# The gates' exponentials moved behind the last convolution activation, the parameter load put first, and two gate rows written in place by VectorE

## The chip, the cores and the metric

The kernel runs on one core of one Trainium2 chip. The metric is the device time of one execution in microseconds (us); lower is better. A core has five engines with queues of their own: TensorE (PE in the profile; its weight loads are PEld), VectorE (DVE), ScalarE (ACT), GpSimd (POOL) and SyncE (SP), which issues most of the transfers. Each engine works through its queue in order, and waits on semaphores for the others.

## The reference

One layer of a hybrid decoder for a prompt of 512 tokens and a sample group of 8 sequences of 8 tokens, which share the weights (576 tokens of width 1024 in all). The layer adds three blocks to x, each with RMS norms around it: a mixer with Mamba-2 heads and mLSTM heads behind one combined input projection, a cross attention to a memory, and a SwiGLU block. The part that matters here is the mixer's beginning:

```python
u = _rms(x) * g_pre_mix
proj = u @ w_in
z, xbc, dt_raw, q, k, v, ig, fg, og = jnp.split(proj, split_at, axis=-1)
xbc, conv_new = causal_conv(xbc, conv_buf, conv_w, conv_b)
xbc = jax.nn.silu(xbc)
dt = jax.nn.softplus(dt_raw.astype(jnp.float32) + dt_bias.astype(jnp.float32))
a = -jnp.exp(a_log.astype(jnp.float32))
y_ssd, h_new = ssd_scan(xs, dt, a, bm, cm, h_ssm)
...
logf = jax.nn.log_sigmoid((fg + b_fgate).astype(jnp.float32))
h_ml, c_new, n_new, m_new = mlstm_scan(q, k, v, i_pre, logf, mc, mn, mm)
```

Both scans go chunk by chunk. Inside them stand running sums of the gates' logarithms (cum, and the mLSTM's running maximum), and exponentials of differences of these sums: decays from a step to its chunk's end, and of a chunk as a whole.

## The kernel before

All of the work is in one function, `build`, over tiles of 128 partitions; features lie on the partitions and the 576 tokens along the free axis. A product of float32 matrices is made of three products of halves: each operand is split into a rounded part and its rest (`uh` and `ul` for the input, `whi` and `wlo` for the weights), and TensorE adds whi·uh, whi·ul and wlo·uh in PSUM (lines 208, 209 and 211 in the helper, 350 to 352 for the first two tiles). Weights come by transfer into `raw`, ScalarE casts them to `whi` (L186), and `wlo` is made by VectorE (L193) or by ScalarE and an accumulating transfer of GpSimd (L190, L191).

**The order.** Most of the program's order on each engine is chosen by the scheduler of the tile framework, which simulates a timeline (`TCOPT = dict(schedule_with_timeline_sim=True)`). Each engine then runs that fixed order. `tc.issue_after(x)` adds an edge that keeps the block's instructions on x's engine behind x in that order, and `tc.high_priority` raises a block's rank. Tiles come from pools with a fixed number of buffers; `MP` takes its PSUM banks from a pool of three, `GP` from another pool of three.

**The start.** VectorE clears `wz`, and TensorE runs `NWARM` = 17 products of 128x256 in bfloat16 on it, whose results nobody reads. Meanwhile SP issues the first transfers in this order: a piece of weights `raws[0]` (L318), the parameters `par` (L320: gains, biases, convolution weights), then the rows of x and further pieces of weights; the first row of x and the first piece of `raws[1]` go through ScalarE's queue. `uh` is x times a gain out of `par` (ScalarE, L333), `ul` the rest (VectorE, L334). The first two weight tiles are multiplied in step with the arrival of x, k by k; the third follows with its weights from L186 and L193.

**The convolution and the gates.** The projection's tiles come in the order: four convolution tiles, the gate tile, one q/k tile, eight more convolution tiles, seven more q/k tiles. `conv_tile` takes a tile out of PSUM (L469, L471), multiplies and adds the four taps (one ScalarE operation, L494, three of VectorE, L496) and ends with two Silu activations (L498, L500). The gate tile goes to `xg` (L448 to L452); from it a long row of VectorE operations makes softplus and the running sums: `pl`, `cum`, `mrw`, `mp`, `sx`, `gpr`. These are rows of 4 or 16 partitions and 576 columns. ScalarE copies them into one stack of rows, `r1`, which is cleared beforehand:

```python
    A.copy(r1[0:16, :], cum[0:16, :])
    A.copy(r1[32:48, :], pl[0:16, :])
    ...
    A.copy(r1[64:68, :], gpr[r4, :])
    A.copy(r1[96:100, :], sx[r4, :])
    A.copy(r2, mrw[r4, :])
```

TensorE transposes `r1` and `r2`, chunk by chunk, into the PSUM tiles `ps_ct` and `ps_ct2` (L589 to L594); copied out, they are `CT`, which has the gates by token. A product with a constant picks each chunk's last token (`ps_en`, L597; `ps_en2`, L604). Out of these come `wend`, `wendm`, `decp`, `scalem` and `expnm`, each by an exponential of ScalarE (L601 to L612). `decp` and `scalem` are read straight from `ps_en`. The whole of this stands under `tc.high_priority(offset=1000)`, so that in the schedule the exponentials stand among the Silus of the last convolution tiles.

**The state-space part.** `ssd_prompt` transposes B and x (`ps_bt`, `ps_xt`), multiplies B and C (`ps_cb`), and makes `xdt` (VectorE, L646), `xe` = `xdt` times `wend` (GpSimd, L650), the chunk states (`ps_h`, L652), the masks `lm` (L672 to L675) and the inner products (`ps_yi`, L682). The projection's q/k tiles, and after them the products of the value projection (`ps_v`, L854), fill TensorE's time between its steps. The list `steps_` ties these value products to steps of `ssd_prompt`: the first 33 stand behind the inner product of its third round.

Everything behind it (output projection, cross attention, SwiGLU) is touched by the change only through the time at which it starts.

Of the kernel before, what the change touches and what calls it, by code (L numbers as in the profile page):

```python
# [14 lines left out]
AF = mybir.ActivationFunctionType  # L15
ALU = mybir.AluOpType
# [4 lines left out]
T = 576  # L21
TP = 512
TS = 64
# [83 lines left out]

CUT = 512
CCUT = 128
NWARM = 17  # L110
NSS = 7
NWX = 3
TCOPT = dict(schedule_with_timeline_sim=True)
# [2 lines left out]
def build(nc, tc, ctx, I, O):  # L116
    V, A, G, S, TE = nc.vector, nc.scalar, nc.gpsimd, nc.sync, nc.tensor
# [35 lines left out]
    par = cp.tile([P, NPAR], F32, name="par")  # L153
# [139 lines left out]
    wendm = ml.tile([P, 5, 4], F32, name="wendm")  # L293
    scalem = ml.tile([P, 4, 4], F32, name="scalem")
# [12 lines left out]
    psw = MP("ps_warm")  # L307
    for _ in range(NWARM):
        mm(psw[:, 0:256], wz[:, 0:128], wz, start=True, stop=True, skip_group_check=True)

    wl = [wp.tile([P, 1024], F32R, name="wlo", tag="wlo", bufs=3) for _ in range(2)]
    RT = {k: wp.tile([P, 3], F32, name=k + "_r", tag=k + "_r") for k in ("px0", "p30", "px1", "p31")}
# [2 lines left out]
    for k in range(KT):  # L315
        if k % 2 == 0:
            c = slice(128 * k, 128 * k + 256)
            S.dma_start(raws[0][:, c], I["win"][1][:, c])  # L318
        if k == 0:
            S.dma_start(par, I["par"])  # L320
        xd = (S if k else A).dma_start(xraw[:, k, :], I["xT"][:, k, :])
        if k % 2 == 0:
            xd = (S if k else A).dma_start(raws[1][:, c], I["win"][2][:, c])
        if k == 0:
            with tc.issue_after(xd.ins), tc.high_priority(offset=300):

                A.activation(sp.tile([P, 1], F32, name="one"), wz[:, 0:1], AF.Exp)

        if k == 0:
            V.tensor_copy(wi[0][0][:, c], raws[0][:, c])  # L330
        for t0, n in ([(0, T)] if k else HALVES):
            ts_ = slice(t0, t0 + n)
            uhk = A.activation(uh[:, k, ts_], xraw[:, k, ts_], AF.Copy, scale=PAR("g_pre", k))  # L333
            ulk = V.scalar_tensor_tensor(ul[:, k, ts_], xraw[:, k, ts_], PAR("g_pre", k), uh[:, k, ts_].bitcast(F32),  # L334
                                         op0=ALU.mult, op1=ALU.subtract)
        if k % 2 == 0:
            for i in range(2):
                with tc.issue_after(uhk.ins), tc.issue_after(ulk.ins):
                    split(wi[i][0][:, c], wi[i][1][:, c], raws[i][:, c], cast=None if k or i else lambda *_: None)
# [81 lines left out]
    wend = bcp.tile([P, 5, 16], F32, name="wend")  # L421
    decp = bcp.tile([P, 4, 16], F32, name="decp")
# [35 lines left out]
    cst = cv.tile([P, 12, NB, 3], F32, name="cst")  # L458
    S.dma_start(cst, I["convst"])

    late_rows, last_in = [], [5]

    def conv_tile(j, dst):

        cb = cv.tile([P, 604], F32, name="cb", tag="cb", bufs=2)
        sm = cb[:, CS:CB].rearrange("p (b t) -> p b t", t=11)

        def ev(t0, n, ps):
            V.tensor_tensor(cb[:, 3 + t0:259 + t0], ps[:, 0:256], rxb[:, t0:t0 + 256], op=ALU.mult)  # L469
            if t0:  # L470
                V.tensor_tensor(sm[:, :, 3:11], ps[:, 256:320].rearrange("p (b t) -> p b t", t=8),  # L471
                                rxb[:, TP:T].rearrange("p (b t) -> p b t", t=8), op=ALU.mult)

        in_tile(1 + j, ev, CUT if j == 4 else 0)
        with ExitStack() as after:
            if 4 <= j < 10:
                for i in range(2 + j, 4 + j):
                    if i > last_in[0]:
                        fetch(i, 0)
                        last_in[0] = i  # L480
                after.enter_context(tc.issue_after(accs[-1].ins))
            if late_rows:
                late_rows.pop()()
            G.memset(cb[:, 0:3], 0.0)
            G.tensor_copy(sm[:, :, 0:3], cst[:, j, :, :])

        def rows_out():
            G.tensor_copy(convo[:, j, 0:3], cb[:, CS - 3:CS])
            G.tensor_copy(convo[:, j, 3:27].rearrange("p (b t) -> p b t", t=3), sm[:, :, 8:11])

        late_rows.append(rows_out)
        e = V
        ac = cv.tile([P, 604], F32, name="ac", tag="ac", bufs=2)
        A.activation(ac[:, 0:600], cb[:, 0:600], AF.Identity, scale=PAR("convw", 4 * j), bias=PAR("convb", j))  # L494
        for k in range(1, 4):
            e.scalar_tensor_tensor(ac[:, 0:600], cb[:, k:600 + k], PAR("convw", 4 * j + k), ac[:, 0:600],  # L496
                                   op0=ALU.mult, op1=ALU.add)
        A.activation(dst[:, 0:TP], ac[:, 0:TP], AF.Silu)  # L498
        sa = ac[:, CS:CB].rearrange("p (b t) -> p b t", t=11)
        A.activation(dst[:, TP:T].rearrange("p (b t) -> p b t", t=8), sa[:, :, 0:8], AF.Silu)  # L500


    qk = SL(1, "qk")
# [37 lines left out]
    r4 = slice(32, 36)  # L541
    r1 = row("r1", 100)
# [4 lines left out]
    i2, mrw, mp = row("i2"), row("mrw", tag="xg"), row("mp", tag="pl")  # L547
    l2, gpr = row("l2", tag="e1"), row("gpr", tag="rmask")
# [10 lines left out]
    V.tensor_copy(mp[r4, 512:576].rearrange("p (c t) -> p c t", t=8), m0.unsqueeze(2).to_broadcast([4, 8, 8]))  # L559
    sx = row("sx", tag="la")  # L560
    V.tensor_tensor(sx[r4, :], cum[r4, :], mrw[r4, :], op=ALU.subtract)
    sx_done = V.tensor_tensor(sx[r4, :], sx[r4, :], mp[r4, :], op=ALU.add)
    V.tensor_tensor(gpr[r4, :], ig[r4, :], cum[r4, :], op=ALU.subtract)
    V.tensor_tensor(gpr[r4, :], gpr[r4, :], mp[r4, :], op=ALU.subtract)
    r2 = row("r2", 4, tag="i2")
    A.copy(r1[64:68, :], gpr[r4, :])
    A.copy(r1[96:100, :], sx[r4, :])
    A.copy(r2, mrw[r4, :])
    V.tensor_copy(cdup, cum[0:16, TP:T].unsqueeze(1).to_broadcast([16, 2, TS]))
    A.copy(mrow, r2[:, TP:T])  # L570
# [2 lines left out]
    for st_, src, n in ((cumst, cum[0:16, :], 16), (sxst, sx[r4, :], 4)):  # L573
        b0 = 32 if n == 4 else 0
        bt, d1 = btt[b0:b0 + n, :], d1t[b0:b0 + n, :]
        G.memset(st_, 0.0)
        V.tensor_copy(bt, src)
        A.copy(st_[0:n, :], bt)
        with tc.issue_after(sx_done.ins):
            V.tensor_tensor(d1, src, bt, op=ALU.subtract)  # L580
        V.tensor_copy(bt, d1)
        A.copy(st_[32:32 + n, :], bt)
        V.tensor_tensor(d1, d1, bt, op=ALU.subtract)
        A.copy(st_[64:64 + n, :], d1)

    with tc.high_priority(offset=1000):
# [11 lines left out]
        en = pse[:, 0:416].rearrange("p (c k) -> p c k", c=4)  # L598
        V.tensor_tensor(wend[:, 0:4, :], en[:, :, 0:16], CT[:, 0:4, 0:16], op=ALU.subtract)
        V.tensor_tensor(wendm[:, 0:4, :], en[:, :, 96:100], CT[:, 0:4, 64:68], op=ALU.add)  # L600
        A.activation(decp, en[:, :, 0:16], AF.Exp)  # L601
        A.activation(scalem, en[:, :, 96:100], AF.Exp)
        pse = MP("ps_en2")
        mm(pse[:TS, 0:104], C32("esamp")[:TS, :], CT[:TS, 4, :], start=True, stop=True)  # L604
        V.tensor_tensor(wend[:TS, 4, :], pse[:TS, 0:16], CT[:TS, 4, 0:16], op=ALU.subtract)
        V.tensor_tensor(wendm[:TS, 4, :], pse[:TS, 96:100], CT[:TS, 4, 64:68], op=ALU.add)
        A.activation(wend[:, 0:4, :], wend[:, 0:4, :], AF.Exp)
        A.activation(wendm[:, 0:4, :], wendm[:, 0:4, :], AF.Exp)
        A.activation(wend[:TS, 4, :], wend[:TS, 4, :], AF.Exp)
        wd = A.activation(wendm[:TS, 4, :], wendm[:TS, 4, :], AF.Exp)  # L610
        with tc.issue_after(wd.ins):
            A.activation(expnm, CT[:, 0:4, 100:104], AF.Exp, scale=-1.0)  # L612
        V.tensor_scalar(ncum, CT[:, 0:4, 0:16], -1.0, None, op0=ALU.mult)
# [1804 lines left out]
```

## Time and profile before

| what | us |
|---|---|
| median of 3 executions | 1080.8 |
| lowest and highest | 1078.0, 1081.1 |
| profiled execution: its own time | 1079.13 |
| profiled execution: span, first to last instruction | 1077.4 |
| busy: TensorE | 1067.5 |
| busy: VectorE | 752.0 |
| busy: ScalarE | 607.8 |
| busy: GpSimd | 231.5 |

A row of the timeline has the start in us from the span's beginning, the time it took, the engine, the line, the operation, out<-in with shapes, and in brackets how long the engine had been idle and what ended that. A row of stretches has for each engine its busy time and, in brackets, the number of instructions, then TensorE's granted clock, the busy share of the transfer engines, and GB/s. A row of the chain has start, time, engine, tile, line and count. A row of the waits has who waited for whom, the sum in us, the times and the longest. Ends of products are modelled, so that products overlap in the records; their starts are what tells the rate.

### The profile page before, as it was taken

Reading aid. Unit: us, or ns where it says so; the run is one execution under the profiler, and the core shown is the slowest. Engines: PE = TensorE matmul, PEld = TensorE weight load, DVE = VectorE, ACT = ScalarE, POOL = GpSimd, SP = SyncE. Lnnn points to the kernel's source line nnn. Section 1 sums busy time; section 2 is a strip of 40 time slices with the busy share of each in tenths; the row PEclk is TensorE's granted clock in tenths of the full one; section 3 lists DMA queues with packets and bytes.
Section 4 is the critical chain, followed back from the end, with each engine's and each line's share of the span. In section 5 each row is a group of like instructions: output and inputs, shape, how many; then the busy total and the mean of one; then the engine's idle time right before and its main releaser. Section 6 shows DMA issues by size and latency. Waiting matters only on the chain.

```text
span 1077.4 us, 20699 instructions
## 1 busy us (share of the span) xinstructions
PE 1067.5 (99%) x8120; PEld 1015.1 (94%) x8120; DVE 752.0 (70%) x1509; ACT 607.8 (56%) x1094; POOL 231.5 (21%) x305
## 2 busy tenths in 40 slices
PE   9999999999999999999999999999999999999997
PEld 8999887778999999999999889999999999999997
DVE  6798775658877775559755555766467887787556
ACT  7778532345654555656555445645566566656653
POOL 0453643313213111000154301100011111111000
PEclk9999999999999999999999999999999999999998
DMA  6787544426655449743468775644476697588532
GB/s 208 164 171 133 159 127 177 147 73 183 191 153 145 111 120 329 254 169 109 147 206 286 268 257 176 241 131 93 136 181 140 155 201 167 116 190 184 130 132 89
DMA packets 58822, 181.76 MB, mean 169 GB/s; under 512 B 6588, under 2 KB 11836, under 8 KB 58212
## 3 DMA queue, kind: packets, MB, share of 16 engines
q1 hardware_dynamic: 42740, 138.06, 39.1%
q0 software_dynamic: 15408, 41.43, 20.0%
q8 instruction: 64, 1.05, 0.4%
q10 hardware_dynamic: 576, 0.95, 0.3%
q14 instruction: 34, 0.28, 0.1%
HBM read 159.75 MB, written 20.65 MB: 167 GB/s over the span
## 4 chain that ended last, share of the span: by engine, by line
PE 93%; DVE 3%; ACT 1%; DMA 1%; issue 1%; POOL 0%; DVEq 0%; SPq 0%; ACTq 0%
PE ps_in L208 6%; PE ps_in L211 6%; PE ps_in L209 6%; PE ps_v L854 5%; PE ps_o L211 3%; PE ps_g L1910 3%; PE ps_g L1909 3%; PE ps_o L209 3%; PE ps_g L1911 3%; PE ps_o L208 3%; PE ps_u L1910 3%; PE ps_u L1911 3%; PE ps_u L1909 3%; PE ps_dn L1909 2%; PE ps_dn L1910 2%; PE ps_dn L1911 2%
## 5 line engine op out<-in xcount | busy, mean ns | idle before, releaser
L211 PE MATMUL ps_in<-uh,wlo 128*128 128x320 f32 (+1 forms) x544 | 161.6, 298 | 0.0
L208 PE MATMUL ps_in<-uh,whi 128*128 128x320 f32 (+1 forms) x544 | 161.6, 297 | 0.0
L209 PE MATMUL ps_in<-ul,whi 128*128 128x320 f32 (+1 forms) x544 | 160.9, 296 | 0.0
L186 ACT CAST whi<-raw 128x1024 fp32r<-128x1024 f32 (+1 forms) x104 | 105.4, 1014 | 96.3 <-PE ps_in L209 30.2
L193 DVE TENSOR_TENSOR wlo<-raw,whi 128x1024 fp32r<-128x1024 f32 (+2 forms) x97 | 94.8, 979 | 61.8 <-ACT whi L186 57.3
L211 PEld LDWEIGHTS ps_in<-uh,wlo 128*128 128x128 f32 x544 | 102.2, 188 | 2.0 <-issue 1.3
L208 PEld LDWEIGHTS ps_in<-uh,whi 128*128 128x128 f32 x544 | 102.3, 188 | 1.5 <-issue 0.8
L209 PEld LDWEIGHTS ps_in<-ul,whi 128*128 128x128 f32 x544 | 102.3, 188 | 0.4
L191 POOL DMA_DIRECT2D wlo<-win x31 | 27.2, 876 | 76.0 <-ACT wlo L190 64.7
L1909 PE MATMUL ps_g<-b,whi 128*128 128x288 f32 x144 | 42.4, 295 | 0.0
L1910 PE MATMUL ps_g<-b,whi 128*128 128x288 f32 x144 | 42.4, 295 | 0.0
L1910 PE MATMUL ps_u<-b,whi 128*128 128x288 f32 x144 | 42.2, 294 | 0.0
L1909 PE MATMUL ps_u<-b,whi 128*128 128x288 f32 x144 | 42.2, 294 | 0.0
L1882 ACT CAST whi<-rawx 128x1024 fp32r<-128x1024 f32 (+1 forms) x26 | 25.7, 987 | 27.7 <-PE ps_dn L1910 13.7
L198 DVE TENSOR_TENSOR wlo<-sw,whi 128x1024 fp32r<-128x1024 f32 (+1 forms) x26 | 29.6, 1140 | 15.5 <-ACT whi L197 15.4
L208 PE MATMUL ps_xo<-qh,whi 128*128 128x288 f32 x128 | 38.4, 302 | 0.1
L211 PE MATMUL ps_o<-mixm_h,wlo 128*128 128x256 f32 (+1 forms) x128 | 37.7, 295 | 0.0
L209 PE MATMUL ps_xo<-ql,whi 128*128 128x288 f32 x128 | 37.7, 296 | 0.0
L209 PE MATMUL ps_o<-mixm_l,whi 128*128 128x256 f32 (+1 forms) x128 | 37.5, 293 | 0.0
L211 PE MATMUL ps_xq<-u2h,wlo 128*128 128x320 f32 (+1 forms) x128 | 37.5, 294 | 0.0
L209 PE MATMUL ps_xq<-u2l,whi 128*128 128x320 f32 (+1 forms) x128 | 37.4, 294 | 0.0
L211 PE MATMUL ps_o<-mixs_h,wlo 128*128 128x320 f32 (+1 forms) x128 | 37.4, 292 | 0.0
(770 smaller groups left out, 3848.6 us busy)
## 6 DMA issues: line engine op xcount, KB each, us to landing
raw<-win SPq DMA_DIRECT2D x35, 512.0 KB, 4.1
raw<-wout SPq DMA_DIRECT2D x17, 512.0 KB, 4.0
raw<-wxq SPq DMA_DIRECT2D x13, 512.0 KB, 4.0
raw<-wgate SPq DMA_DIRECT2D x13, 512.0 KB, 3.6
raw<-wup SPq DMA_DIRECT2D x13, 512.0 KB, 5.0
wlo<-win POOLq DMA_DIRECT2D x24, 256.0 KB, 5.1
kva<-vc SPq DMA_DIRECT2D x11, 512.0 KB, 6.5
raw<-wv SPq DMA_DIRECT2D x10, 512.0 KB, 4.1
```

The costliest lines, as they stand in the source:

```text
L186: casts.append(A.copy(hi[:, :n], raw[:, :n]))
L191: accs.append(G.dma_start(lo[:, a:b], src[:, a:b], accum_op=ALU.add))
L193: e.tensor_tensor(lo[:, a:b], raw[:, a:b], hi[:, a:b].bitcast(F32), op=ALU.subtract)
L198: (eng or V).tensor_tensor(lo, src, hi.bitcast(F32), op=ALU.subtract)
L208: mm(ps, wh, ah, start=i == 0, stop=False)
L209: mm(ps, wh, al, start=False, stop=False)
L211: m = mm(ps, tiles[order[c]][1], xh(order[c], t0, n), start=False, stop=c == len(tiles) - 1)
L854: mm(ps, a, b, skip_group_check=True, **kw)
L1882: A.copy(s.h3[:, s.all], s.r2[:, s.all])
L1909: mm(ps, wh, b[0][k], start=start and k == 0, stop=False, skip_group_check=True)
L1910: mm(ps, wh, b[1][k], start=False, stop=False, skip_group_check=True)
L1911: m = mm(ps, wl, b[0][k], start=False, stop=k == nk - 1, skip_group_check=True)
```

## The change

It has three parts. The transfer of `par` is issued on SP ahead of the first piece of weights instead of behind it, and there are 21 warm-up products instead of 17. The last step of `sx` and `gpr` is written by VectorE straight into `r1`, without ScalarE's two copies; `sx` itself, which a later stack of bfloat16 rows needs, is finished after that by one more VectorE operation, and the edge that held the bfloat16 stacks behind `sx` holds them behind the rows now. And the exponentials are put behind the last Silu in ScalarE's order: `decp` behind the last Silu, the others behind `decp`.

```diff
-NWARM = 17
+NWARM = 21
...
     for _ in range(NWARM):
         mm(psw[:, 0:256], wz[:, 0:128], wz, start=True, stop=True, skip_group_check=True)
+    S.dma_start(par, I["par"])
...
         if k % 2 == 0:
             c = slice(128 * k, 128 * k + 256)
             S.dma_start(raws[0][:, c], I["win"][1][:, c])
-        if k == 0:
-            S.dma_start(par, I["par"])
         xd = (S if k else A).dma_start(xraw[:, k, :], I["xT"][:, k, :])
...
-    late_rows, last_in = [], [5]
+    late_rows, last_in, silus = [], [5], []
...
         A.activation(dst[:, 0:TP], ac[:, 0:TP], AF.Silu)
         sa = ac[:, CS:CB].rearrange("p (b t) -> p b t", t=11)
-        A.activation(dst[:, TP:T].rearrange("p (b t) -> p b t", t=8), sa[:, :, 0:8], AF.Silu)
+        silus.append(A.activation(dst[:, TP:T].rearrange("p (b t) -> p b t", t=8), sa[:, :, 0:8], AF.Silu))
...
     V.tensor_tensor(sx[r4, :], cum[r4, :], mrw[r4, :], op=ALU.subtract)
-    sx_done = V.tensor_tensor(sx[r4, :], sx[r4, :], mp[r4, :], op=ALU.add)
+    V.tensor_tensor(r1[96:100, :], sx[r4, :], mp[r4, :], op=ALU.add)
     V.tensor_tensor(gpr[r4, :], ig[r4, :], cum[r4, :], op=ALU.subtract)
-    V.tensor_tensor(gpr[r4, :], gpr[r4, :], mp[r4, :], op=ALU.subtract)
+    r1_done = V.tensor_tensor(r1[64:68, :], gpr[r4, :], mp[r4, :], op=ALU.subtract)
+    with tc.issue_after(r1_done.ins):
+        V.tensor_tensor(sx[r4, :], sx[r4, :], mp[r4, :], op=ALU.add)
     r2 = row("r2", 4, tag="i2")
-    A.copy(r1[64:68, :], gpr[r4, :])
-    A.copy(r1[96:100, :], sx[r4, :])
     A.copy(r2, mrw[r4, :])
...
-        with tc.issue_after(sx_done.ins):
+        with tc.issue_after(r1_done.ins):
             V.tensor_tensor(d1, src, bt, op=ALU.subtract)
...
-        A.activation(decp, en[:, :, 0:16], AF.Exp)
-        A.activation(scalem, en[:, :, 96:100], AF.Exp)
+        with tc.issue_after(silus[-1].ins):
+            dx = A.activation(decp, en[:, :, 0:16], AF.Exp)
+        with tc.issue_after(dx.ins):
+            A.activation(scalem, en[:, :, 96:100], AF.Exp)
...
-        A.activation(wend[:, 0:4, :], wend[:, 0:4, :], AF.Exp)
-        A.activation(wendm[:, 0:4, :], wendm[:, 0:4, :], AF.Exp)
-        A.activation(wend[:TS, 4, :], wend[:TS, 4, :], AF.Exp)
-        wd = A.activation(wendm[:TS, 4, :], wendm[:TS, 4, :], AF.Exp)
+        with tc.issue_after(dx.ins):
+            A.activation(wend[:, 0:4, :], wend[:, 0:4, :], AF.Exp)
+            A.activation(wendm[:, 0:4, :], wendm[:, 0:4, :], AF.Exp)
+            A.activation(wend[:TS, 4, :], wend[:TS, 4, :], AF.Exp)
+            wd = A.activation(wendm[:TS, 4, :], wendm[:TS, 4, :], AF.Exp)
```

## The prediction

> **What bounds the kernel now.** I read the share of each engine first, then the waits of TensorE, then the same engine in stretches.
>
> ```profile
> PE 1067.5 (99%) x8120; PEld 1015.1 (94%) x8120; DVE 752.0 (70%) x1509; ACT 607.8 (56%) x1094; POOL 231.5 (21%) x305
> ```
> ```profile
> PE ps_warm L309 <- DVE wz L306: 1.1, 1, 1.1
> PE ps_in L350 <- ACT uh L333: 1.0, 1, 1.0
> PE ps_ct L589 <- ACT r L567: 0.3, 1, 0.3
> ```
> ```profile
> 0.00:10.00 10.00, 7.90 (x33) 6.32 (x34) 4.74 (x13) 5.52 (x11) 0.98 (x9) 1.00 0.83 257
> 10.00:20.00 10.00, 10.00 (x77) 10.00 (x77) 7.65 (x13) 7.69 (x13) 0.76 (x2) 1.00 0.89 300
> ...
> 1060.00:1077.40 17.40, 10.34 (x91) 10.05 (x89) 9.74 (x21) 5.51 (x12) 0.00 (x0) 0.84 0.33 118
> ```
> TensorE is busy for all but 9.9 of 1077.4 us. Of these, 7.1 lie in the last 17.4 us, which the change leaves alone; 2.1 lie ahead of the first real product and 0.3 at the gates' transposes ps_ct. Those last two places are the ones the change touches. No other engine's time counts unless TensorE waits for it. The second column of the stretches shows something else: 33 products in the first 10 us against 77 in the next, although TensorE is called busy in both. The reason is in the timeline of the start:
>
> ```profile
> 0.74 0.39 SPq L318 DMA_DIRECT2D raw<-win  x1
> ...
> 1.06 3.81 PE L309 MATMUL ps_warm<-wz 128*128 128x256 bf16 x17 [1.06 <-DVE wz L306]
> ...
> 4.50 0.29 DVE L330 CAST whi<-raw 128x256 fp32r<-128x256 f32 x1 [3.50 <-DMA raw<-win]
> ...
> 5.35 0.96 ACT L333 ACTIVATE uh<-xraw,par 128x256 fp32r<-128x256 f32 x2 [2.19 <-DMA par<-par]
> ...
> 5.91 1.09 PE L350 MATMUL ps_in<-uh,whi 128*128 128x256 f32 x2 [1.04 <-ACT uh L333]
> ...
> 7.01 0.41 PE L350 MATMUL ps_in<-uh,whi 128*128 128x256 f32 x1
> ...
> 7.23 0.41 PE L351 MATMUL ps_in<-ul,whi 128*128 128x256 f32 x1
> ...
> 13.38 0.28 PE L351 MATMUL ps_in<-ul,whi 128*128 128x256 f32 x1
> ...
> 13.49 0.28 PE L352 MATMUL ps_in<-uh,wlo 128*128 128x256 f32 x1
> ```
> The same 256 columns start 0.22 us apart at 7.0 (7.01, 7.23) and 0.11 us apart at 13.4 (13.38, 13.49): TensorE starts at half rate. The 17 warm-up products, 3.81/17 = 0.224 us each, were half rate throughout. Then it idled 1.04 us for the parameters, and it was still at half rate at 7.2.
>
> The Trainium skill, "TensorE: Matmul & The Clock Gate", Part 1, says that the clock goes to full rate only after a whole free-running window of about 3.4 us in which TensorE is busy. The trace agrees in that 3.81 us of work followed by a hole of 1.04 us was not enough; by the rule, unbroken work from 1.06 would reach full rate between 1.06 + 3.4 = 4.5 and 1.06 + 6.8 = 7.9, an estimate, and the gain would be the one worked out below, because its ceiling comes from elsewhere.
>
> **Edit 1: parameters first, 21 warm-up products.** The load of the parameters moves from second to first place on SP's queue, ahead of a weight load; the transfers behind keep their places.
>
> ```profile
> 1.19 4.07 DMA par<-par
> ```
> The parameters landed at 1.19 + 4.07 = 5.26, and ScalarE's first uh started at 5.35. Issued one place earlier, 0.45 us (1.19 less 0.74), I expect them at 4.8; if the input row, whose landing has no row, is later, the gain goes to 0. The weight load then lands 0.45 later, at 4.95 instead of 4.50, and its cast of 0.29 ends at 5.24, when uh is nearly ready too. Four more warm-up products cost 4 × 0.224 = 0.90 us and end at 1.06 + 21 × 0.224 = 5.76, against data for the first real product at about 5.45. They cost up to 0.3 us of waiting, but TensorE still starts 0.15 earlier than 5.91, and the hole of 1.04 is gone.
>
> What that brings: 33 − 17 = 16 real products took 5.91 to 10.0, 4.09 us; at the next stretch's 10/77 = 0.130 us they are 2.08 us. So full rate from the start is worth 2.0 us, and nothing if TensorE still speeds up as late as now. What is late next caps it:
>
> ```profile
> 17.33 1.23 DVE L193 TENSOR_TENSOR wlo<-raw,whi 128x1024 fp32r<-128x1024 f32 x1 [1.24 <-ACT whi L186]
> ```
> ```profile
> 20.61 0.31 PE L352 MATMUL ps_in<-uh,wlo 128*128 128x320 f32 x1
> ```
> The next unit's low weights are ready at 18.56, and TensorE comes for them at 20.61 + 0.15: they allow 2.2 at most, since they hang on a transfer and on ScalarE (the wait in their row), which do not move. I take 2.0, between 0 and 2.2.
>
> **Edit 2: two rows written by VectorE.** It removes two ScalarE copies and adds one VectorE operation (sx is still finished for its bfloat16 stack, but after the rows).
>
> ```profile
> 76.70 0.77 DVE L561 TENSOR_TENSOR sx<-cum,mrw 4x576 f32<-4x576 f32 x1
> ...
> 77.96 0.75 DVE L564 TENSOR_TENSOR gpr<-gpr,mp 4x576 f32<-4x576 f32 x1
> 78.74 0.84 DVE L496 SCALAR_TENSOR_TENSOR ac<-cb,par,ac 128x600 f32<-128x600 f32 x1
> ```
> ```profile
> 78.74 0.67 ACT L566 COPY r<-gpr 4x576 f32<-4x576 f32 x1 [1.18 <-DVE gpr L564]
> 79.44 1.05 ACT L186 CAST whi<-raw 128x1024 fp32r<-128x1024 f32 x1
> 80.52 0.67 ACT L567 COPY r<-sx 4x576 f32<-4x576 f32 x1
> ```
> ```profile
> 80.69 0.31 PE L208 MATMUL ps_in<-uh,whi 128*128 128x320 f32 x1
> 81.33 0.28 PE L589 MATMUL ps_ct<-c,r 100*128 100x100 f32 x1 [0.34 <-ACT r L567]
> ```
> Now the rows are whole at 80.52 + 0.67 = 81.19, and the transpose starts at 81.33, 0.64 after the product ahead of it, where 0.13 is usual (10/77, above): 0.5 us are lost. After the change VectorE needs two operations of 0.75 behind sx's end at 77.47: whole at 79.0, or at 80.3 with the convolution work that stands between them now (the 0.49 up to 77.96, and the 0.84 at 78.74). That is 0.9 to 2.2 earlier, so the 0.5 goes. But TensorE comes 2.0 earlier: if VectorE's chain started no sooner, it would wait 80.3 − 78.85 = 1.5 here. The chain's start, though, hung on TensorE:
>
> ```profile
> 39.55 0.43 ACT L448 COPY xg<-ps_in 40x320 f32<-40x320 f32 x1 [0.43 <-PE ps_in L445]
> ```
> so it moves most of the way with it. I take 0.4 of the 0.5; the bounds are +0.5 and −1.0. The added 0.75 on VectorE falls behind the rows; queued behind it are the convolution's multiply-adds (the 0.84 row is one), which nothing on TensorE waited for before; the same 0.75 is the most it can cost.
>
> **Edit 3: exponentials behind the last Silu.** The seven exponentials stand between two table loads, ahead of the last Silus:
>
> ```profile
> 91.45 1.28 ACT L607 ACT_TABLE_LOAD   x1
> ...
> 93.39 0.20 ACT L612 ACTIVATE expnm<-CT 128x16 f32<-128x16 f32 x1
> 93.59 1.28 ACT L498 ACT_TABLE_LOAD   x1
> ...
> 105.99 0.24 ACT L500 ACTIVATE xs<-ac 128x64 f32<-128x64 f32 x1
> ```
> ```profile
> 106.44 1.04 POOL L650 TENSOR_TENSOR xe<-xdt,wend 128x512 f32<-128x512 f32 x1 [0.71 <-DVE xdt L646]
> ```
> Two loads go, 2.56 us of ScalarE; the third, for the next exponential, only moves forward. TensorE does not wait for ScalarE here, so this is worth nothing by itself.
>
> The Trainium skill, "ScalarE: Activation LUTs", What ACT_TABLE_LOAD costs, gives about 2.66 us for each switch, with a drain; by it 5.3 us of ScalarE would go. The rows show 1.28 and the next exponential right behind, so the rows decide, and the sum is the same by both.
>
> The price is that wend, decp and scalem come after 106.23 + 1.28 + 0.3 to 0.9 = 107.8 to 108.4 instead of 93. The first reader is xe on GpSimd at 106.44, delayed 1.4 to 2.0. Behind the exponentials on ScalarE stand the copies of ps_bt and ps_cb and a cast of weights, up to 1.28 + 0.9 = 2.2 later; the first of them is the other operand of xe's product:
>
> ```profile
> 109.25 1.02 PE L652 MATMUL ps_h<-xe,btok 128*128 128x512 f32 x2
> ```
> xe ended at 107.48, 1.77 before this: the slack covers nearly all. Behind it the state-space chain feeds the value products, which are ordered behind its third inner product:
>
> ```profile
> 161.44 1.29 DVE L675 TENSOR_TENSOR lm<-lm,cbs 128x512 f32<-128x512 f32 x2
> ```
> ```profile
> 162.84 1.03 PE ps_yi L682 x16
> ...
> 164.91 2.09 PE ps_v L854 x9
> ```
> There the slack is 162.84 − 162.73 = 0.1, and the projection products that fill the gaps have just run out. Whatever the chain loses against TensorE beyond its slack becomes idle time: 0 to 2.0. I take 0.8, since the first link is covered and the last is not.
>
> **Sum**, against the profiled execution (1079.1 us, 1.7 more than its span): 2.0 + 0.4 − 0.8 = 1.6 off, 1077.5. The four executions known (1080.8, 1081.1, 1078.0, 1079.1) average 0.6 above that one, so I add 0.6: **1078.1**.
>
> **Rivals.** *All is kept (1076.0).* The chain moves with TensorE and the schedule fills around it: 2.0 + 0.5 off 1079.1 is 1076.6, and if speeding up late, by a varying amount, is also what makes the middle run 1.7 slower, up to 1.7 more comes off the runs: 1075 to 1076.6. For it: TensorE has no other wait. Against: the 0.1 at the third inner product. *TensorE does not speed up earlier, or VectorE's chain swallows it (1079.5).* Then the edits do not do what they say: 0 to 0.5 off the average, 1079.7. *Slower (1085): the bank of ps_en.* ps_en lies in one of three PSUM banks taken in turn (ps_ct, ps_ct2, ps_en, ps_en2, ps_bt, ps_cb), so ps_cb needs its bank, now held until decp and scalem are read.
>
> ```profile
> 99.43 1.06 PE L635 MATMUL ps_cb<-bc 128*128 128x128 f32 x8
> ```
> If the scheduler leaves ps_cb near 99.4, TensorE stands there until about 107.9, 8.5 us, and 2.4 off against 8.5 on gives 1085. It decides once ps_cb stands over 5.6 us ahead of the last exponential in true time (2.4 + 3.2). For it: TensorE is in order and everything queues behind ps_cb. Against: the order is made by a timeline simulation that knows the dependence, and its products came 1.8 us after their data at ps_h, so it is not optimistic here.
>
> **How the numbers follow.** A measurement of this kernel tells about 0.3%, 3.2 us, from no change: faster is below 1077.6, slower above 1084.0. The forecast has 0.45: a third of it falls below 1077.6 (0.15), the rest within. All kept 0.25, all of it faster. No earlier full rate 0.10, within. Slower 0.20, nearly all above 1084. Faster 0.40, same 0.40, slower 0.20. The range, 1074.5 to 1083.5, takes in the first three and leaves out most of the last.
>
> **What would show it.** Right: 21 warm-up products end where the first L350 starts, no wait on uh; products 0.11 us apart before 8 us; the first unit with L193's weights starts near 18.7; ps_ct released by VectorE with no wait; one table load between the Silus and the first exponential. Wrong: half rate still at 10 us; a new wait of ps_cb or ps_h on ScalarE, or idle TensorE ahead of the first ps_v.

## The result, and the profile after

The change made the kernel slower: 1086.65 us median of 6 runs (1084.88 to 1088.24) against 1079.27 for the kernel before (1077.57 to 1081.1), a ratio of 1.0068 with a 95% interval of 1.0054 to 1.0083. The forecast was 1078.1, its range ended at 1083.5. The profiled execution of after took 1087.2 us, its span 1085.4. One execution of one kernel further down, the repaired edit 2 without the exponentials, took 6024 us and is left out of the range given for it, though not out of its median.

TensorE is still busy for 99% of the span. Its waits, from the waits of after:

```profile
PE ps_hu L798 <- DVE h L799: 1.7, 1, 1.7
PE ps_hu L798 <- ACT bm L793: 1.4, 1, 1.4
PE ps_warm L309 <- DVE wz L306: 1.1, 1, 1.1
PE ps_os L1446 <- ACT kva L1471: 0.6, 1, 0.6
PE ps_in L208 <- ACT la L448: 0.6, 1, 0.6
PE ps_ct L588 <- DVE r L561: 0.6, 1, 0.6
PE ps_yi L684 <- DVE lm L677: 0.4, 1, 0.4
```

The wait for `uh` is gone. In its place stand five new ones, none of them in work that was edited, and the one at ps_ct has grown from 0.3 to 0.6. The start does what it was meant to do (timeline and stretches of after):

```profile
1.06 4.08 PE L309 MATMUL ps_warm<-wz 128*128 128x256 bf16 x21 [1.06 <-DVE wz L306]
4.10 0.96 ACT L332 ACTIVATE uh<-xraw,par 128x256 fp32r<-128x256 f32 x2
5.13 0.51 PE L349 MATMUL ps_in<-uh,whi 128*128 128x256 f32 x2
...
16.62 1.23 DVE L193 TENSOR_TENSOR wlo<-raw,whi 128x1024 fp32r<-128x1024 f32 x1 [1.56 <-ACT whi L186]
```
```profile
0.00:10.00 10.00, 8.94 (x57) 7.62 (x58) 5.35 (x13) 6.09 (x12) 0.98 (x9) 1.00 0.84 277
```

Real products begin at 5.13 instead of 5.91, and 57 products instead of 33 fall into the first 10 us (21 and 17 of them warm-up products). At the gates' transposes TensorE is 1.85 us ahead of before (79.48 against 81.33). The loss is made later. These are a stretch of before, and then two of after, around the first value products; the second column has TensorE's busy time and count, the first figure behind the last bracket its granted clock:

```profile
160.00:170.00 10.00, 10.00 (x67) 8.08 (x65) 7.32 (x16) 4.53 (x7) 1.03 (x1) 1.00 0.67 257
```
```profile
160.00:170.00 10.00, 7.82 (x45) 6.38 (x45) 8.44 (x19) 3.20 (x5) 1.01 (x1) 0.74 0.64 189
170.00:180.00 10.00, 10.00 (x46) 6.79 (x44) 5.61 (x14) 2.82 (x4) 1.20 (x2) 0.92 0.38 141
```

In after TensorE stands still for 2.2 us of the first stretch, and the clock falls in both. The timeline of TensorE shows it product by product, first the first value product of before, then after:

```profile
164.66 0.48 PE L854 MATMUL ps_v<-whi,uh 128*128 128x512 f32 x1
```
```profile
162.48 0.31 PE L211 MATMUL ps_in<-uh,wlo 128*128 128x320 f32 x1
164.53 0.56 PE L798 MATMUL ps_hu<-stb,bm 96*128 96x512 f32 x1 [1.74 <-DVE h L799]
165.53 1.98 PE L684 MATMUL ps_yi<-lm,xdt 128*64 128x128 f32 x16 [0.44 <-DVE lm L677]
...
169.06 0.77 PE L856 MATMUL ps_v<-whi,uh 128*128 128x512 f32 x1
169.63 0.63 PE L856 MATMUL ps_v<-whi,ul 128*128 128x512 f32 x1
170.05 0.63 PE L856 MATMUL ps_v<-wlo,uh 128*128 128x512 f32 x1
...
171.94 0.39 PE L856 MATMUL ps_v<-whi,ul 128*128 128x512 f32 x1
172.17 0.39 PE L856 MATMUL ps_v<-wlo,uh 128*128 128x512 f32 x1
```

The last projection product starts at 162.48. The next one, 2.05 us later, waited until VectorE had added an earlier product out of its PSUM bank to a state (its pool has two banks, and ps_hs holds one); the inner product behind it waited for a mask. The first value product comes at 169.06, where before, whose real products start 0.8 us later, had it at 164.66. And at 169.6 products of 512 columns start 0.42 us apart, at 172 0.23: after the idle time TensorE ran at half rate, from 164.82 to 171.64 by the record of the granted clock, 6.83 us in which half, 3.4 us, is lost.

A sum over the starts of all products between 20 and 1060 us (counting how much later each starts than the columns of the one ahead need at full rate, 512 columns in 0.23 us, where that is over 0.3 us) gives 8.1 us in after and 0.5 in before. So 7.6 us more idle and 3.4 lost at half rate, less 2.7 gained at the start (at ps_ss, 23.83 against 26.54, the best lead), make 8.3, where the spans differ by 8.0.

### The profile page after: what moved, and what is told of

The parts are those of the page before. It is cut to its first block, busy times and chain, and to the rows that moved or that the text cites. A ratio compares the mean times of both kernels' runs of the same rounds, so it can differ in the third digit from the quotient of the medians.

```text
span 1085.4 us, 20697 instructions
## 1 busy us (share of the span) xinstructions
PE 1071.6 (99%) x8124; PEld 1016.6 (94%) x8124; DVE 752.5 (69%) x1510; ACT 603.6 (56%) x1090; POOL 233.9 (22%) x305
## 4 chain that ended last, share of the span: by engine, by line
PE 83%; DMA 6%; DVE 5%; ACT 3%; issue 2%; POOL 0%; SPq 0%; DVEq 0%; ACTq 0%; POOLq 0%
PE ps_in L208 5%; PE ps_in L209 5%; PE ps_in L211 5%; PE ps_v L856 4%; PE ps_g L1912 3%; PE ps_u L1912 3%; PE ps_g L1911 3%; PE ps_u L1913 3%; PE ps_g L1913 3%; PE ps_u L1911 3%; PE ps_dn L1911 2%; PE ps_dn L1912 2%; PE ps_dn L208 2%; PE ps_dn L1913 2%; PE ps_dn L211 2%
## 5 line engine op out<-in xcount | busy, mean ns | idle before, releaser
L193 DVE TENSOR_TENSOR wlo<-raw,whi 128x1024 fp32r<-128x1024 f32 (+2 forms) x97 | 96.7, 999 | 62.7 <-ACT whi L186 61.6
L208 PE MATMUL ps_o<-mixm_h,whi 128*128 128x256 f32 (+1 forms) x128 | 37.4, 292 | 0.1
```

Of the source, the lines that this page charges most:

```text
L193: e.tensor_tensor(lo[:, a:b], raw[:, a:b], hi[:, a:b].bitcast(F32), op=ALU.subtract)
L208: mm(ps, wh, ah, start=i == 0, stop=False)
```

## The experiments

Each kernel was timed in five rounds beside the kernel before, whose medians in the three groups of runs were 1079.66, 1079.62 and 1079.64. After was timed in a group of its own, with 1079.27 for the kernel before, so a gain against after is some 0.4 us more than the two medians say. Ratios go by all runs and not by the medians alone.

**The three parts one by one.** Each diff of the change was applied alone, and the first two together.

> The kernel before with the first part alone: parameters first, 21 warm-up products. Theory A (the state-space chain sets the pace where the filling products run out): the start gives the 2.7 us that the changed kernel had gained at ps_ss, but the chain starts with the last Silu and does not move by as much, so part of it comes back as idle time ahead of the first ps_v: 1076.5 to 1079, and a wait of under 1.5 us there. Theory B (any change of the order shuffles the schedule and puts waits at places of no relation): anywhere from 1076 to 1084, with the waits elsewhere.

> The kernel before with the second part alone: two rows of r1 written by VectorE. Theory A: the wait of 0.5 us at ps_ct goes and nothing else changes, 1078.5 to 1079.5. Theory B: waits at new places, up to 4 us slower.

> The kernel before with the third part alone: the exponentials behind the last Silu. Theory A: the bank of ps_en is held some 13 us longer, ps_xt and with it the chain of states come later while TensorE runs ahead with projection products; these run out ahead of the third inner product, TensorE idles 1 to 3 us there and drops to half rate for up to 6.8 us: 1081.5 to 1085.5. Theory B: no idle time at that place, and the slower time of the change needs all three parts together.

> The changed kernel without its third part: first and second part together. Theory A: the start's gain and the rows' gain, less what the chain gives back: 1076 to 1078.5, no drop of the rate between 100 and 300 us. Theory B: as slow as the change, 1084 or more, if the first two parts alone shuffle the schedule so that the filling products run out.

| kernel | median us (range) | ratio to before, interval |
|---|---|---|
| edit 1, start | 1077.24 (1076.55 to 1079.56) | 0.9984, 0.9975 to 0.9993 |
| edit 2, rows | 1086.11 (1084.62 to 1087.42) | 1.0064, 1.0051 to 1.0077 |
| edit 3, exponentials | 1087.0 (1086.09 to 1088.46) | 1.0071, 1.0058 to 1.0085 |
| edits 1 and 2 | 1082.15 (1081.22 to 1084.48) | 1.0028, 1.0017 to 1.004 |

The start alone is a gain, the other two lose each by itself, and the losses do not add up. Edit 1 came out as both its theories allowed, edits 1 and 2 between their two. Edit 2 lost more than either of its theories had. Edit 3 showed what its theory A named, TensorE idle ahead of the third inner product (1.75 us up to 165.18, 0.50 up to 166.19) and half rate from 166.17 on, and took 1.5 us more than that theory's range.

Edit 1 leaves the order of all engines as it was behind the first few instructions, and its waits of TensorE are these, all of them:

```profile
PE ps_warm L309 <- DVE wz L306: 1.1, 1, 1.1
PE ps_in L208 <- ACT la L448: 0.3, 1, 0.3
PE ps_ct L588 <- ACT r L566: 0.2, 1, 0.2
```

Behind the start there is half a microsecond in which TensorE waits for anything. Whatever edits 2 and 3 do on VectorE and ScalarE, they had no more than that to gain. Both change the order that the scheduler chooses from the gates on: in the traces 138 of TensorE's 8120 products stand at another place with edit 2, 403 with edit 3. The new orders have waits. Edit 2 alone waits 0.8 us at ps_hu (to 177.90) and 1.2 at ps_yi (to 179.64), and has two windows of 3.41 us at half rate, from 84.26 and from 179.83. In edits 1 and 2, whose profile is 4.7 us longer than that of edit 1, the same two waits make 2.0 of it, a window of half rate at 82 us 1.7, and ps_ct 0.4.

Edit 2 alone, and edits 1 and 2, also have a change on ScalarE that nobody had asked for: the scheduler put a Silu between the exponentials, so that four table loads (1.28 us each) stand there instead of two. In edits 1 and 2 the last Silu starts at 107.99, with edit 1 alone at 104.38. What this adds to the lateness of the state-space part was not measured by itself.

**Is any new order a loss?** A copy that has no purpose was added to the kernel before:

```diff
+    A.copy(r1[96:100, :], sx[r4, :])
```

> The kernel before, with ScalarE's copy of the row sx into r1 done twice (0.67 us more on ScalarE, at the gates' transposes); nothing of the change is in it. The scheduler's order on TensorE differs from before in 27 places. Theory A (the loss needs the change's own work: late exponentials or rows): as before, 1079.7 within 1, apart from up to 0.7 at ps_ct; no waits of TensorE over 1 us between 160 and 215 us. Theory B (any disturbance of the scheduler's order loses, because the order before happens to have no waits): 1082 to 1087, with waits of ps_yi, ps_hu or ps_os that before does not have, and perhaps a window of half rate behind them.

1080.65 us (1079.27 to 1082.46), ratio 1.0011, 1.0002 to 1.002. In the traces the order on TensorE differs from that of before by more than with edit 2 (216 products, at 41 places; the expectation counted 27), and yet there is no wait of TensorE between 160 and 215 us. So not every new order loses. The kernel is a useful control for the next theory too, as the timeline of its VectorE and GpSimd shows:

```profile
145.25 4.63 DVE L676 TENSOR_TENSOR lm<-lm,cbs 128x512 f32<-128x512 f32 x2
```
```profile
145.04 9.51 POOL L794 TENSOR_TENSOR h<-h,vt 128x1024 f32<-128x1024 f32 x4 [2.59 <-PE ps_hs L786]
```

Two mask products take 4.63 us here, against 1.29 for two at 161.44 in before. They lie beside GpSimd's state products. TensorE had other work there and nothing waited.

**VectorE beside GpSimd.** In edits 1 and 2 together the fourth round's masks meet them, and there TensorE waits. In the experiment GpSimd's state products of the third round are held behind the masks; the order on the other engines stays the same but for single rows.

```diff
-                    G.tensor_copy(sd.tile([P, 1], F32, name="lm0"), lm[:, 0:1])
+                    held.append(G.tensor_copy(sd.tile([P, 1], F32, name="lm0"), lm[:, 0:1]))
...
-            with tc.issue_after(mults[7].ins) if b == 2 else ExitStack():
+            with tc.issue_after(held[0].ins) if b == 2 else ExitStack():
```

> Edits 1 and 2 without the exponentials, and GpSimd's two state products of the third round held behind the fourth round's mask, so that they no longer run beside VectorE's two mask products (2.23 and 1.82 us there, 0.68 each in before, where nothing ran beside them). The order of every other engine is that of edits 1 and 2. Theory C (two engines' contention makes the wait): the mask products take 0.7 each, the 1.7 us wait of ps_yi at 176 goes, the window of half rate at 82 stays, 1079 to 1080.8 beside 1082.2. Without contention: the mask products keep 1.8 to 2.2 and the time stays at 1082 to 1083, or is later still if the state is needed sooner than it comes now.

Edits 1 and 2 (timeline of VectorE, of GpSimd, of TensorE):

```profile
173.34 2.23 DVE L674 TENSOR_TENSOR lm<-lm,cbs 128x512 f32<-128x512 f32 x1
175.49 0.68 DVE L796 TENSOR_TENSOR h<-h,ps_hu 128x512 f32<-128x512 f32 x1
176.09 1.82 DVE L674 TENSOR_TENSOR lm<-lm,cbs 128x512 f32<-128x512 f32 x1
```
```profile
173.08 4.28 POOL L792 TENSOR_TENSOR h<-h,vt 128x1024 f32<-128x1024 f32 x2 [5.21 <-PE ps_hs L784]
```
```profile
177.96 1.09 PE L681 MATMUL ps_yi<-lm,xdt 128*64 128x128 f32 x16 [1.24 <-DVE lm L674]
```

With the state products held:

```profile
173.37 0.68 DVE L674 TENSOR_TENSOR lm<-lm,cbs 128x512 f32<-128x512 f32 x1
...
174.74 0.69 DVE L674 TENSOR_TENSOR lm<-lm,cbs 128x512 f32<-128x512 f32 x1
```
```profile
175.67 3.83 POOL L792 TENSOR_TENSOR h<-h,vt 128x1024 f32<-128x1024 f32 x2
```
```profile
175.64 1.09 PE L681 MATMUL ps_yi<-lm,xdt 128*64 128x128 f32 x16
```

The masks take 0.68 and 0.69 instead of 2.23 and 1.82, and the inner product starts at 175.64 instead of 177.96, without a wait. The median falls from 1082.15 to 1080.33 (1079.03 to 1081.91), as expected. Not all of that need be the masks'. The first profile has a window of half rate at 82 us, long before the edit can act; the second has none, came 1.5 us sooner to ps_xt, and then stood 1.1 us at ps_h. Executions with the same mean granted clock, 0.996, took 1081.61 to 1083.98 (four, edits 1 and 2) and 1080.33 and 1081.91 (two, held): on average 1.35 us less, about the 1.24 us that the inner product no longer waits. With so few executions this is a rough figure.

The rows show what the slowing depends on. The sum of the state at 175.49, in the middle of GpSimd's time, takes 0.68 as ever: one of its operands is in PSUM. The masks take both from SBUF. The Trainium skill, "SBUF — State Buffer", Who interferes with whom, says that a VectorE instruction with two SBUF inputs gets its second input through a read interface that it shares with GpSimd, and that the shared pair of ports is an exclusive lock. The trace agrees: the first of the two state products ran from 173.08 for its usual 1.94, to 175.02, and the mask of 173.34 ended at 175.57, 0.55 behind it; the second took 2.38, to 177.36, and the mask of 176.09 ended at 177.91, again 0.55 behind.

**The same in after.** There it is the weight casts of the value projection that meet GpSimd. This experiment leaves out fifteen of sixteen heads of the state products of the first two rounds:

```diff
-                G.tensor_tensor(hn, hn, decs[:, :, bb:bb + 1].to_broadcast([P, 16, 64]), op=ALU.mult)
+                nh = 1 if b < 2 else 16
+                G.tensor_tensor(hn[:, 0:nh, :], hn[:, 0:nh, :], decs[:, 0:nh, bb:bb + 1].to_broadcast([P, nh, 64]), op=ALU.mult)
```

> After, with GpSimd's four products of the sampled states of the first two rounds (128x1024 each, 9.4 us in all beside VectorE's two weight casts at 154.6) cut to one of their sixteen heads; this part of the state output is left out. Nearly the same order everywhere else (TensorE 29 rows, VectorE 8, ScalarE none). Theory C (VectorE is slowed by GpSimd beside it, and that makes TensorE stand): the two casts take 1.2 each instead of 2.3, the chain behind them comes 2.2 earlier, the 2.05 and 1.0 us of idle TensorE at 162 to 165 fall below 1 together and the half rate with them: 1081 to 1083.5. Theory A alone (the chain is late for its length and its late start, whatever runs beside it): idle places and time as in after, 1085.5 to 1087.5.

1081.03 us (1079.92 to 1083.34), 5.6 below after. VectorE in after, and then here:

```profile
154.55 4.61 DVE L193 TENSOR_TENSOR wlo<-raw,whi 128x1024 fp32r<-128x1024 f32 x2
```
```profile
153.76 1.22 DVE L193 TENSOR_TENSOR wlo<-raw,whi 128x1024 fp32r<-128x1024 f32 x1
...
155.67 1.23 DVE L193 TENSOR_TENSOR wlo<-raw,whi 128x1024 fp32r<-128x1024 f32 x1 [0.28 <-ACT whi L186]
```

Two casts beside GpSimd: 4.61. Without it: 1.22 and 1.23. VectorE has 2.2 us more ahead of the state sums and masks, and in this kernel neither ps_hu nor ps_yi waits at 162 to 166, and no half rate follows there. The chain itself was no sooner: ps_h starts at 113.39 here and at 112.21 in after. The experiment shortens GpSimd's own products too, but these were not what was waited for in after: the last of them ended at 158.07, and the sum that ps_hu needed came at 163.80, in its turn on VectorE.

What sets after apart is the place of this loss and not its size. In before the same four products of GpSimd, from 143.61 to 151.68, slowed a mask (147.80, 2.08 instead of 0.68) and a cast, 2.5 us in all:

```profile
150.40 2.35 DVE L193 TENSOR_TENSOR wlo<-raw,whi 128x1024 fp32r<-128x1024 f32 x1
```

There it was some ten microseconds ahead of the third inner product, and TensorE had projection products to run.

**The order of the casts, the work to fill with, and the clock.** Three more edits of after. The casts of the first two value units later on VectorE:

```diff
-            with tc.issue_after(added[0].ins) if g == 0 and u < 2 else ExitStack():
+            with tc.issue_after(mults[5].ins) if g == 0 and u < 2 else ExitStack():
```

Value products from the second round's inner product on:

```diff
-              (159, inner[4]), (200, inner[5]), (10000, None), (0, inner[2])]
+              (159, inner[4]), (200, inner[5]), (10000, None), (0, inner[1])]
```

Products whose results nobody reads, ahead of the value products:

```diff
+NKEEP = 20
...
+    psw = GP("ps_keep")
+    for _ in range(NKEEP):
+        mm(psw[:, 0:256], U(0, 0, 128), U(0, 0, 256), start=True, stop=True, skip_group_check=True)
```

> After, with the low halves of the first two units of value weights (two casts on VectorE, 9.2 us of busy time at 154.6 to 163.8 in after) ordered behind the eighth-to-last mask product instead of behind the first of the added states, so that the state-space chain's last steps are not queued behind them on VectorE. Theory C (VectorE is the engine that is late there, slowed by GpSimd's state products beside it): the 2.0 and 1.0 us of idle TensorE at 162 and 165 shrink below 1 together, the half rate goes or halves, 1081 to 1084. Theory A in the prediction's form (the chain is late because it started late): unchanged idle places, 1086 to 1087.5. If the value products then wait for their weights instead: idle time moves to ps_v, 1086 to 1090.

> After, with the first 33 value products tied to the inner product of the second round instead of the third, so that TensorE has work it may do while it waits for the third round's masks. Theory A (filling work has run out where the chain is late): the 2.05 and 1.0 us of idle TensorE at 162 to 165 go, with the half rate behind them (3.4), 1080 to 1083; the value weights are then needed some 5 us sooner, and if VectorE cannot make them beside GpSimd's products (theory C), the wait comes back at ps_v with 1 to 3 us: 1083 to 1086.

> After, with 20 products of 128x256 whose results nobody reads ahead of the value products, where TensorE stands idle (162 to 166 us). They cannot bring the data sooner; they only keep TensorE from idling. If the half rate for 6.8 us behind the idle places comes from the idleness and costs what the count of products says (half of 6.8, 3.4 us): that stretch runs at full rate and the time falls to 1083 to 1085, the waits of ps_yi and ps_hu in the same places giving back 0 to 1 of it to the products' own 2.2 us of work. If the half rate is only how the idleness is seen and has no price of its own (the value products wait for something else as well): 1086 to 1088.5. Theory B is told apart by neither, as only TensorE's order moves (16 places).

The casts later: 1085.08 (1082.4 to 1088.78). Value products sooner: 1084.45 (1083.51 to 1085.14). Both remove the idle time at 162 to 166, and both have this in its place ten microseconds later (waits of the two kernels, in this order), with half rate behind it, 3.41 us from 177.99 and 6.83 us from 175.02:

```profile
PE ps_hs L787 <- DMA h<-h: 3.8, 1, 3.8
```
```profile
PE ps_hs L787 <- DMA h<-h: 2.4, 1, 2.4
```

That is the load of the third round's state. It uses the buffers of the first round, which must be summed by VectorE and stored first. So in after this chain is late as well (the second half of the load is issued at 173.82 there, at 171.58 with the casts later); the time lost from 162 on had hidden it. The first time lies between the expectations, the second in the one that had a wait at ps_v; but in both the new wait is another, which none of them had named.

The idle products: 1085.15 (1082.96 to 1086.11), 1.5 below after, where 1083 to 1085 was expected. The profiled execution, with 1082.96 the best of five, shows the mechanism:

```profile
160.00:170.00 10.00, 9.87 (x73) 8.69 (x72) 8.09 (x19) 3.20 (x5) 1.76 (x2) 1.00 0.64 189
```

The clock stays at 1.00, and the first value product starts at 166.78 instead of 169.06. VectorE's sums and masks lie 0.6 us sooner in this execution (the mask of 164.80 at 164.16), so 1.6 of the 2.3 us is the clock's. The other executions have a mean granted clock of 0.996 to 0.998: the drop comes elsewhere in some of them, which fits the smaller gain of the median, but only one was traced.

**Edit 2's rows.** In edits 1 and 2, and in after, TensorE waits 0.6 at ps_ct. The timeline of VectorE in after says why:

```profile
76.29 0.75 DVE L563 TENSOR_TENSOR r<-gpr,mp 4x576 f32<-4x576 f32 x1
77.05 0.75 DVE L579 TENSOR_TENSOR d1t<-cum,btt 16x576 f32<-16x576 f32 x1
...
78.58 0.75 DVE L561 TENSOR_TENSOR r<-sx,mp 4x576 f32<-4x576 f32 x1
```

The edge that holds the bfloat16 stack (L579) back is tied to the gpr row, but the scheduler issues that row first and the sx row last, with the stack and a convolution operation between them. The rows are whole at 79.33; with edit 1 alone ScalarE's copies had them at 79.56. Here the edge is tied to the sx row:

```diff
-        with tc.issue_after(r1_done.ins):
+        with tc.issue_after(r1_sx.ins):
             V.tensor_tensor(d1, src, bt, op=ALU.subtract)
```

> Edits 1 and 2, without the exponentials, and with the edge that holds back the bfloat16 stacks (L579) on the sx row of r1, which VectorE writes last, instead of on the gpr row. In edits 1 and 2 as they were the scheduler put the stack's 0.75 us operation between the two rows, so that the rows were whole at 79.46 against 79.56 with ScalarE's copies, and TensorE stood 0.75 us at ps_ct. Now: rows whole near 78.7 or earlier, no wait at ps_ct. The order of TensorE is near that of edit 1 (92 rows moved instead of 352). If the wait and the reordering were what edits 1 and 2 lost against edit 1 (4.9 us): 1077 to 1078.5. If every changed order pays: 1080 to 1083.

> After, with the same edge on the row written last. The exponentials stay behind the last Silu. If edit 3 is enough by itself to spoil the state-space part (edit 3 alone: 1087.0): the 0.75 us at ps_ct go and nothing else does, 1085 to 1086.5, with idle TensorE at 160 to 166 and at 212 as in after. If edit 2's disturbance is the cause in after: 1077 to 1080.

Without the exponentials 1080.19 (1078.76 to 1080.96; ratio 1.0005, 0.9996 to 1.0014), with them 1085.4 (1083.37 to 1088.71). Without them the rows are whole at 78.65, 0.7 sooner than in after, and TensorE waits no less than before the repair:

```profile
78.80 0.28 PE L588 MATMUL ps_ct<-c,r 100*128 100x100 f32 x1 [0.80 <-DVE r L561]
```

The scheduler had moved the transposes forward along with the rows. The gain of 2 us against edits 1 and 2 lies elsewhere: in the new order the exponentials stand between two table loads again, and the two waits near 177 are gone. The lower expectation, from 1077 on, held in neither kernel; the other did, but the wait at ps_ct that was to go stayed in both. The repaired edit 2 still loses 3 us against edit 1 (2.7 in the profiles); new waits explain some 1.8 of these, 0.6 each at ps_ct and ps_os and the rest in the first 40 us, and what remains I have not placed. With the exponentials the idle places of after stay, at 164, 166 and 212, and one at 178 is new; edit 3 alone has those at 163, 166 and 212 too.

## Why the prediction was wrong, point by point

**Edit 1: right.** 2.0 off was predicted, 1.7 measured (by the ratio, 0.16%, 0.07 to 0.25; also 1.7 between the profiles, 2.4 between the medians). The parts of it were less exact and differ from execution to execution. With edit 1 alone the parameters were there by 4.3 instead of 4.8, the first real product started at 5.40 instead of 5.76, and full rate came at 6.5. In after these were 3.8, 5.13 and 4.4, so that there the last warm-up products were already fast. The first unit with L193's weights was ready at 18.10 (in after 17.85) instead of 18.56, and nothing waited for it. In the ten traced executions with edit 1 full rate began between 3.9 and 6.7; the estimate by the rule of the Trainium skill ("TensorE: Matmul & The Clock Gate", Part 1) was 4.5 to 7.9. So it held but for its lower end: in the kernel with the casts later a step from 0.50 to 3.91, whose first 0.56 us lay ahead of the first product, was enough.

**Edit 2: the wrong sign.** I took 0.4 off, from 0.5 off to 1.0 on. TensorE's wait at ps_ct rose from 0.3 to 0.6, and edit 2 alone cost 0.64%, 6.9 us. The step that failed is the one that counted the rows and ps_ct alone and left the rest of the order as it was. I had written down that convolution work might stand between the rows, but costed it as if its place were given; the scheduler put other work there as well, moved the transposes forward, and split the exponentials by a Silu. What was paid came later: 2.0 us of waits for VectorE near 178, and half rate. The edge tied to the wrong row was there to be read in the diff.

**Edit 3: the place right, the path and the size wrong.** That the two table loads bring TensorE nothing was right: one load is left, at 103.70, and the time did not fall. That the chain's delay becomes idle TensorE ahead of the first value product was the step that set the result, and the sign named for it came. Its size, 0.8 between 0 and 2.0, is the term that failed: edit 3 alone cost 0.71%, 7.7 us. These rows of after answer to the ones that I used:

```profile
105.18 0.26 ACT L609 ACTIVATE wend<-wend 128x64 f32<-128x64 f32 x1
```
```profile
109.25 1.38 POOL L652 TENSOR_TENSOR xe<-xdt,wend 128x512 f32<-128x512 f32 x1
```
```profile
112.21 1.02 PE L654 MATMUL ps_h<-xe,btok 128*128 128x512 f32 x2
```

wend is ready 2.4 us sooner than I had put it, yet xe starts 2.8 later than before and ps_h 3.0 later, 4.5 against edit 1 alone (107.67). So the delay is not that of wend. It comes by a PSUM bank. Four of the tiles here share the pool of three: ps_en, ps_bt, ps_cb and then ps_xt. In before the transposes of x into ps_xt started at 100.32; in after they start at 106.31. Edit 3 alone shows what they wait for (rows of before, then TensorE and ScalarE with edit 3 alone):

```profile
100.32 0.60 PE L644 MATMUL ps_xt<-c,xs 128*128 128x128 f32 x4
```
```profile
106.87 0.60 PE L647 MATMUL ps_xt<-c,xs 128*128 128x128 f32 x4
```
```profile
106.27 0.18 ACT L604 ACTIVATE scalem<-ps_en 128x16 f32<-128x16 f32 x1
...
106.89 0.57 ACT L635 COPY btok<-ps_bt 128x512 f32<-128x512 f32 x1
107.35 0.58 ACT L642 COPY cbs<-ps_cb 128x512 f32<-128x512 f32 x1
```

At 106.87 neither ps_bt nor ps_cb has been copied out, so only the bank of ps_en can be free, and that is held until scalem is read, at 106.45. In after the same reading ends at 105.29. In the new order the transposes of x, and the chain behind them, stand later on TensorE, with projection products ahead, so that it does not stand still there. VectorE's xdt then also stands behind a weight cast that waits until 107.76 for ScalarE. From there GpSimd's state products came 5.1 us later (148.68 against 143.61), which put the two weight casts beside them; VectorE lost 2.2 directly ahead of the sums and masks of the third round; TensorE's other work had ended at 162.8; it waited 1.7 and 0.4 in two places, and half rate took 3.4 more. I had worked out the slack of the chain in the order of before, and bounded the loss by the delay of one operation. What was missing is that holding ps_en delays ps_xt, that the order behind it would be a new one, that VectorE's durations depend on what GpSimd does beside them, and that idle time has a price above its own length. The trace of before showed the third of these, in a row that I did not read (its neighbours take 0.68):

```profile
147.80 2.08 DVE L675 TENSOR_TENSOR lm<-lm,cbs 128x512 f32<-128x512 f32 x1
```

**The rival "slower, 1085"** had the right bank and the wrong tile. ps_cb started at 98.16 in after, with ps_en still to be read for 7 us, so it does not need that bank; ps_xt does. And TensorE did not stand for 8.5 us at the bank, but for about two at the far end of the chain. That its 1085 came near the time is luck.

**What stays open.** Why the scheduler's order for edits 2 and 3 is worse than its order for the useless copy was not separated further; as far as the runs show, a loss needs both, work on VectorE and GpSimd that meet, and a place at which TensorE has nothing else to do. Before and the copy have the first without the second. How much of the chain's delay with edit 3 is the bank's, and how much the new order's, was not separated either: no run gives ps_en a bank of its own.

The best kernel is edit 1 alone, 1077.24 us, below before and after.

## What to carry to other kernels

Before moving work off an engine, look whether the bottleneck waits for it anywhere: here edit 1 alone left half a microsecond of such waits behind the start, and the two edits that could at best remove them cost several. Where a scheduler makes the order, an edit to an idle engine is an edit to the whole order behind it; look which PSUM bank a delayed reader goes on holding, tie edges to the operation that is issued last, and compare TensorE's list of waits before and after, not the busy shares. Keep VectorE's operations with two SBUF operands away from GpSimd's where TensorE has nothing to fill with.

## What the runs showed of the hardware that was not expected

TensorE fell to half rate with less idle time than I had thought it needed: in after it was idle for 1.7 us between 162.8 and 164.5, ran projection products at full speed before that, and the clock dropped at 164.82. Between the start and the last 20 us, all drops seen last 3.41 us or twice that, and their ends lie on one grid of 3.413 us in each execution (in before full rate lasted 1061.545 us, 311.0 such steps). In after the step that ended with the drop, 161.40 to 164.82, held 1.7 us of waiting; in edits 1 and 2 a step with 1.4 us of it, 173.95 to 177.36, was followed by no drop. At the start, 0.56 us ahead of the first product did not keep a step from counting, as said above; in edit 3 alone a hole of 0.8 us did, in the step from 2.33 to 5.74, and full rate came one step later. A threshold was not measured. In edits 1 and 2 a drop came at 81.79 behind the gates' small transposes and a wait of 0.6; the same order without the drop, in the kernel with the state products held, ran 68 products between 80 and 90 us where this one ran 57 (stretches of the two):

```profile
80.00:90.00 10.00, 10.00 (x57) 8.96 (x57) 9.72 (x22) 8.33 (x13) 3.18 (x9) 0.83 0.68 65
```
```profile
80.00:90.00 10.00, 10.00 (x68) 8.94 (x68) 9.72 (x22) 8.31 (x13) 3.18 (x9) 1.00 0.73 63
```

Eleven products at 10/68 us are 1.6 us, the price of one such step, which one execution of this order paid and another did not.
